# Fetching every token row of an expert block from HBM, one block ahead, in place of picking half of them on chip

## Chip, cores and metric

One core of one Trainium2 chip runs the whole kernel in one launch. The metric is device time in microseconds (us). The kernel before was run three times: 1874.18, 1876.4 and 1895.7 us, median 1876.4 us.

## What is computed

The reference is one layer of a diffusion backbone on 512 latent tokens of width 1024 with 256 context tokens: a mixer (RWKV-7 and HGRN2 heads, output projection, gated residual), then routed and shared SwiGLU experts, another gated residual, and a final RMSNorm. The change lies in the routed experts alone. There, each token goes to 8 of 64 experts, an expert has two 1024x256 matrices (gate, up) and one 256x1024 (down), and the gated results are summed per token:

```python
def _swiglu(x, wg, wu, wd):
    return (jax.nn.silu(x @ wg) * (x @ wu)) @ wd
...
def _moe(h, router_w, router_b, wg, wu, wd, sg, su, sd):
    ...
    _, top_e = lax.top_k(sel, TOP_K)
    gate = jnp.take_along_axis(scores, top_e, axis=1)
    gate = gate / jnp.sum(gate, axis=-1, keepdims=True) * ROUTE_SCALE
    ...
    def step(out, inp):
        tok, gw, e = inp
        y = _swiglu(h[tok], wg[e], wu[e], wd[e]) * gw[:, None].astype(h.dtype)
        return out.at[tok].add(y), None
    routed, _ = lax.scan(step, jnp.zeros_like(h), (tok_buf, gate_buf, blk_e))
    return _swiglu(h, sg, su, sd) + routed
```

Everything is float32; 64 experts of 3 MB each have to be read once.

## The kernel before, in words

The program runs the mixer first (to about 1010 us of the span), then norm, router and shared expert, then the **expert stage**, from about 1095 us to the end.

**Blocks.** Experts are ranked by how many tokens they got; the four experts 0 to 3 of fixed number (NP = 4) come first, since their weights can be loaded before the ranking is known. The work is cut into 46 blocks of at most 128 token rows: a block holds 128 rows of one expert, or 64 rows of each of two, or 96 rows of one and 32 of another. The kinds are interleaved, so three blocks in a row mostly need five experts.

**One block** (the loop over `blocks`, from line 1828):
- `next_list` (`lists`, lines 1621 to 1643) makes the token list of a later block: VectorE (DVE) builds a 0/1 matrix `sel`, four small matmuls and three DVE instructions give the list `lv`, and line 1641 writes it as integers `li` (column 0: rows to read, column 1: rows to add to). There are four `li` buffers, so a new list waits until the scatter that used the list four blocks earlier has landed.
- `front` makes `xT`, the block's token rows transposed and modulated. Most blocks **gather**: GpSimd (POOL) issues an indirect DMA (line 1747) of 128 rows of 4 KB from the DRAM copy `H2_d` into one of two `xg` buffers; TensorE (PE) transposes it with 8 matmuls (line 1753); ScalarE (ACT) writes `xT` (line 1458). The 16 even blocks 12 to 42 (`ONPE`, line 26) instead **pick on chip**: 96 bf16 matmuls (line 1742) multiply `sel` with `h2p`, which holds all 512 rows in three bf16 parts in SBUF.
- `h2_parts` (lines 1725 to 1731) fills `h2p` during blocks 4 to 7 (`HB`): per 128 rows one DMA into an `xg` buffer (`hr`), two ACT copies and two DVE subtractions.
- `ffn_in` (line 1473): 16 to 64 matmuls of 512 columns into `p_gu`. Then `back` for the block before: silu on ACT (1479), product `av` on DVE (1481), transposes on PE (1485), copy on ACT (1487), `ffn_out` (1492) into `p_y`.
- `add_rows`: DVE scales `p_y` into `rows` (1693), POOL issues the indirect **scatter** that adds the 128 rows to `ACC` in DRAM (1694). A scatter waits for the one before it, since both add to the same tensor.

**Weights.** SyncE's queue (SP) carries the loads, three DMAs of 1 MB per expert (line 1378), in the blocks' order. A load is issued only when the second DMA before it has landed (LAG = 2) and when its buffer is free. `wgu` is free after the block's `ffn_in`, `wd` after its `ffn_out`, and those run after the next block's `ffn_in`. Experts 0 to 3 fill the four buffers of pool `wl`; after that line 1717 chooses the pool by a counter:

```python
pl = wl if nload[0] % (NWL + NWR) else wr
nload[0] += 1
```

With NWL, NWR = 4, 1 each load takes the buffer of the expert five loads earlier. A pool hands out its own buffers in turn (`wl` four, `wr` one).

Instruction order on each engine is set by a scheduler from the program's order and its dependences. DVE, POOL, ACT, PE and the SP queue each run their instructions strictly in order.

Of the kernel before, what the change touches and what calls it, by code (L numbers as in the profile page):

```python
# [8 lines left out]
F32 = mybir.dt.float32  # L9
FR = mybir.dt.float32r  # L10
BF = mybir.dt.bfloat16
I32 = mybir.dt.int32
U8 = mybir.dt.uint8
AF = mybir.ActivationFunctionType
OP = mybir.AluOpType
PSUM = bass.MemoryType.PSUM

D = 1024
# [2 lines left out]
NT = SEQ + CTX  # L21
NCH = NT // 64
NCC = CTX // 64
NWL, NWR = 4, 1
LAG = 2
ONPE = range(12, 44, 2)
HB = 4
NP = 4


# [16 lines left out]
def hybrid_layer(ctx, tc, x, c, xctx, c_ctx, w_mod, b_mod, norm1_g, norm2_g, w_in, rw_conv, rw_w0, rw_w2,  # L47
# [3 lines left out]
    nc = tc.nc  # L51
    act, dve, pool, pe = nc.scalar, nc.vector, nc.gpsimd, nc.tensor

    def bc(ap, shape):
        return ap.to_broadcast(shape)
# [17 lines left out]
    def prw(name):  # L73
        turn[0] += 1
        return psb("45"[turn[0] % 2], name)
# [40 lines left out]
    for n in (64, 32):  # L116
        t = const.tile([128, NT // n, n], BF, name=f"rs{n}")
# [100 lines left out]
    sel = const.tile([128, 2], F32)  # L218
# [15 lines left out]
    def dt(name, shape):  # L234
        return dram.tile(list(shape), F32, name=name)
# [13 lines left out]
    H2_d = dt("h2", (NACC, D))  # L249
# [56 lines left out]
    with es:  # L306
        ssx = const.tile([128, 6, 2], F32)
        for t in range(6):
# [6 lines left out]
            for h in range(2):  # L315
                pt = prw("p_xt")
                for q in range(4):
                    kt = h * 4 + q
# [4 lines left out]
        for m in range(4):  # L323
# [3 lines left out]
            for h in range(2):  # L327
                wm = mp.tile([128, 4, 512], F32, name="wm", bufs=4)
                nc.sync.dma_start(wm, dram2(w_mod, m * 512 + h * 512 * 6144, [[6144, 128], [128 * 6144, 4], [1, 512]]))
                for kt in (0, 2, 1, 3):  # L330
                    g = 2 * h + kt // 2
                    pe.matmul(pm[32 * g:32 * g + 32, :], sil[:, 4 * h + kt, :], wm[:, kt, :], start=(kt % 2 == 0),
                              stop=(kt % 2 == 1))
# [887 lines left out]
    def bcast_row(dst, t, off, n):  # L1221
        nc.sync.dma_start(dst, dram2(t, off, [[0, 128], [1, n]]))
# [53 lines left out]
    start = tc.cur_priority  # L1276
# [95 lines left out]
    def load(er, pl):  # L1372

        wgu = pl.tile([128, 2, 2048], F32, name="wgu")
        wd = pl.tile([128, 2048], F32, name="wd")
        for dst, src in ((wgu[:, 0], exp_w_gate), (wgu[:, 1], exp_w_up), (wd, exp_w_down)):
            v = src.rearrange("o e a b -> (o e) (a b)")
            i = nc.sync.dma_start(dst, v[bass.ds(er, 1), :].rearrange("o (p f) -> (o p) f", p=128)).ins

            if len(flight) >= LAG:  # L1380
                tc.add_manual_dep(i, flight[-LAG].name, mybir.DependencyInfo(
                    mybir.DependencyClass.Sync, mybir.DependencyReason.DATA), reason="loads in flight")
            flight.append(i)
        return wgu, wd, i
# [58 lines left out]
    def pst(tag, n, name, w=512):  # L1443
        return psc[0].tile([128, w], F32, name=name, tag=tag, bufs=n)
# [4 lines left out]
    def pss_(tag, name):  # L1449
        psm[tag].append(psm[tag].pop(0))  # L1450
        return psm[tag][-1]

    def modulate(dst, pt, h, eng=act):

        for kt in range(4 * h, 4 * h + 4):
            v = pt[:, (kt - 4 * h) * 128:(kt - 4 * h) * 128 + 128]
            if eng is act:
                act.activation(dst[:, kt, :], v, AF.Identity, scale=s2c[:, kt:kt + 1], bias=sh2c[:, kt:kt + 1])  # L1458
            else:
                dve.tensor_scalar(dst[:, kt, :], v, s2c[:, kt:kt + 1], sh2c[:, kt:kt + 1], op0=OP.mult, op1=OP.add)  # L1460
# [36 lines left out]
    for t in range(4):  # L1497
# [11 lines left out]
        for h in range(2):  # L1509
            pt = pst("pt", 2, "p_h2")  # L1510
# [115 lines left out]
    def lists(parts, kind, rp=RP, rv=RV):  # L1626

        sel = late.tile([128, 4, 128], BF, name="sel", bufs=3)
        pl_ = pss_("li", "p_list")
        p0 = 0  # L1630
        for r, s0, n in parts:
            dve.tensor_tensor(sel[:, :, p0:p0 + n], bc(io[:, None, s0:s0 + n], [128, 4, n]),
                              bc(rp[:, :, r:r + 1], [128, 4, n]), OP.is_equal)
            for t in range(4):
                pe.matmul(pl_[p0:p0 + n, 6 * t:6 * t + 6], sel[:, t, p0:p0 + n], rv[:, t, r], start=True, stop=True)
            p0 += n
        lv = late.tile([128, 8], F32, name="lv", bufs=4)
        dve.tensor_reduce(lv[:, 0:6], pl_[:, 0:24].rearrange("p (t f) -> p f t", t=4), mybir.AxisListType.X, OP.add)
        dve.scalar_tensor_tensor(lv[:, 6:7], lv[:, 2:3], nbp, lv[:, 0:1], op0=OP.mult, op1=OP.add)
        li = late.tile([128, 2], I32, name="li", bufs=4)  # L1640
        dve.scalar_tensor_tensor(li, bc(lv[:, 6:7], [128, 2]), lv[:, 1:2], bpr[:, kind], op0=OP.add, op1=OP.add)  # L1641
        dve.tensor_reduce(lv[:, 7:8], lv[:, 3:6], mybir.AxisListType.X, OP.add)
        return li, lv[:, 7:8], sel


    h64 = lambda a, b: [(a, slice(0, 64)), (b, slice(64, 128))]
# [12 lines left out]
    blocks = [(parts, b, i == 0) for group in order + final for i, (parts, b) in enumerate(group)]  # L1659
    listed = []  # L1660

    def next_list():
        if len(listed) < len(blocks):
            parts, b, _ = blocks[len(listed)]
            s0 = 128 if B2 <= b < BP else 0
            kind = 0 if len(parts) == 1 else 1 if b < BM else 2
            listed.append(lists([(r, s0, s_.stop - s_.start) for r, s_ in parts], kind))
# [33 lines left out]
    wr = fd.enter_context(tc.tile_pool(name="wr", bufs=NWR, side="right", reuse_waits="tile"))  # L1701
    mw = fd.enter_context(tc.tile_pool(name="mw", bufs=2, reuse_waits="tile"))
# [10 lines left out]
    def weights(r):  # L1713

        if r >= 64 - NP:
            return sload[r - 64 + NP][0:2]
        pl = wl if nload[0] % (NWL + NWR) else wr
        nload[0] += 1
        *w, i = load(expert(r), pl)
        last.append(i)  # L1720
        return w

    h2p = mw.tile([128, 3, 4, D], BF, name="h2p", bufs=1)

    def h2_parts(t):

        hr = mw.tile([128, D], F32, name="hr", tag="xg", bufs=2)
        nc.sync.dma_start(hr, H2_d[t * 128:t * 128 + 128, :])
        for i in range(2):
            act.activation(h2p[:, i, t], hr, AF.Copy)  # L1730
            dve.tensor_tensor(hr if i == 0 else h2p[:, 2, t], hr, h2p[:, i, t], OP.subtract)

    def front(tok, sel=None):
        xT = mw.tile([128, 8, 128], F32, name="xT")
        if sel is not None:
            for h in range(2):
                pt = pst("pt", 2, "p_xs")
                for q in range(4):
                    kt = h * 4 + q
                    for i in range(3):  # L1740
                        for t in range(4):
                            pe.matmul(pt[:, q * 128:q * 128 + 128], h2p[:, i, t, kt * 128:kt * 128 + 128], sel[:, t],  # L1742
                                      start=(i == 0 and t == 0), stop=(i == 2 and t == 3))
                modulate(xT, pt, h)
            return xT
        xg = mw.tile([128, D], FR, name="xg", bufs=2)
        pool.indirect_dma_start(out=xg.bitcast(F32), out_offset=None, in_=H2_d,  # L1747
                                in_offset=bass.IndirectOffsetOnAxis(ap=tok, axis=0))
        for h in range(2):
            pt = psc[0].tile([128, 512], FR, name="p_xg", tag="pt", bufs=2)  # L1750
            for q in range(4):
                kt = h * 4 + q
                pe.transpose(pt[:, q * 128:q * 128 + 128], xg[:, kt * 128:kt * 128 + 128], identr)  # L1753
            modulate(xT, pt.bitcast(F32), h)
        return xT
# [69 lines left out]
        nc.sync.dma_start(X_d, xs.rearrange("p i t f -> p (i t f)"))  # L1825

    held = {}
    for i, ((parts, b, first), (li, g, sel)) in enumerate(zip(blocks, listed)):
        if i == 2:
            overflow()  # L1830
        if HB <= i < HB + 4:
            h2_parts(i - HB)
        if i == len(blocks) - 4:
            fr = rows[:, 3]
            bcast_row(fr, final_norm_g, 0, D)
        if first:
            held = {}
        for r, _ in parts:
            if r not in held:
                held[r] = weights(r)  # L1840
        next_list()
        xT = front(li[:, 0:1], sel if i in ONPE else None)
        hv = [(s_, (lambda kt, xT=xT, s_=s_: xT[:, kt, s_]), held[r]) for r, s_ in parts]
        pg = ffn_in(hv, mw)
        if pend:
            back(*pend)
        pend = (pg, hv, g, li[:, 1:2])
# [5 lines left out]
    def extra(i):  # L1853
        er = nc.sync.value_load(xrow[0:1, bass.ds(i, 1)], min_val=0, max_val=63)
        lx = mw.tile([128, 4, 2], F32, name="lx", bufs=1)
        nc.sync.dma_start(lx, X_d[:, bass.ds(i * 8, 8)].rearrange("p (t f) -> p t f", f=2))
        rv = mw.tile([128, 4, 1, 6], BF, name="rv", bufs=1)
        dve.tensor_copy(rv, RV[:, :, 0:1])
        parts3(rv, lx[:, :, 1:2])
        li, g, _ = lists([(0, 0, 128)], 0, lx, rv)  # L1860
        xT, w = front(li[:, 0:1]), load(er, wr)[0:2]
        hv = [(full, lambda kt: xT[:, kt, :], w)]
        back(ffn_in(hv, mw), hv, g, li[:, 1:2])

# [44 lines left out]
```

## Time and profile before

| | |
|---|---|
| profiled execution | 1872.8 us, its span 1871.0 us |
| runs | 1874.18, 1876.4, 1895.7 us |
| PE busy | 1667.0 us (89%), 10155 matmuls |
| DVE, ACT, POOL busy | 751.0, 618.0, 397.2 us |
| granted TensorE clock, mean | 0.896 |
| DMA moved | 401.72 MB, mean 215 GB/s |
| gathers in the expert stage | 30, median 7.7 us to landing |
| scatters | 46, median 11.0 us to landing |

A busy share is a mean over stages with different limits. In the expert stage the slices of the page show which engine is full where; a wait then shows what ended last. Times in the rows count from the span's start.

### The profile page before, as it was taken

Reading aid. Unit: us, or ns where it says so; the run is one execution under the profiler, and the core shown is the slowest. Engines: PE = TensorE matmul, PEld = TensorE weight load, DVE = VectorE, ACT = ScalarE, POOL = GpSimd, SP = SyncE. Lnnn points to the kernel's source line nnn. Section 1 sums busy time; section 2 is a strip of 40 time slices with the busy share of each in tenths; the row PEclk is TensorE's granted clock in tenths of the full one; section 3 lists DMA queues with packets and bytes.
Section 4 is the critical chain, followed back from the end, with each engine's and each line's share of the span. In section 5 each row is a group of like instructions: output and inputs, shape, how many; then the busy total and the mean of one; then the engine's idle time right before and its main releaser. Section 6 shows DMA issues by size and latency. Waiting matters only on the chain. (4 is left out here: it accounts for less than half of the span.)

```text
span 1871.0 us, 26459 instructions
## 1 busy us (share of the span) xinstructions
PE 1667.0 (89%) x10155; PEld 994.6 (53%) x10155; DVE 751.0 (40%) x1722; ACT 618.0 (33%) x1286; POOL 397.2 (21%) x372
## 2 busy tenths in 40 slices
PE   5988989999779999989899997988879999999883
PEld 3756677676567776555445543434334544454431
DVE  3665595755847335433344633311112121212113
ACT  5464435426224435342132423321112222222121
POOL 2234222313313124232123011210111111111111
PEclk9976899989867997868799998998889999999997
DMA  7323445546456435453443688799997899999995
GB/s 267 92 59 100 136 136 156 166 112 171 131 152 186 147 119 172 145 171 118 131 146 119 252 302 272 248 322 334 343 302 252 300 339 343 339 328 333 341 340 169
DMA packets 200256, 401.72 MB, mean 215 GB/s; under 512 B 41804, under 2 KB 132009, under 8 KB 175168
## 3 DMA queue, kind: packets, MB, share of 16 engines
q1 hardware_dynamic: 188768, 360.05, 55.9%
q0 software_dynamic: 11360, 39.96, 9.6%
q8 instruction: 81, 1.33, 0.3%
q14 instruction: 47, 0.39, 0.1%
HBM read 323.66 MB, written 73.15 MB: 212 GB/s over the span
## 5 line engine op out<-in xcount | busy, mean ns | idle before, releaser
L1473 PE MATMUL p_gu<-wgu,xT 128*32 128x512 f32 (+2 forms) x1424 | 353.7, 621 | 16.6 <-DMA wgu<-in_exp_w_up_dram 15.9
L1473 PEld LDWEIGHTS p_gu<-wgu,xT 128*32 128x32 f32 (+2 forms) x1424 | 125.9, 143 | 202.4 <-issue 178.9
L1492 PE MATMUL p_y<-wd,at 128*32 128x512 f32 (+2 forms) x744 | 198.0, 621 | 4.8 <-ACT at L1487 3.6
L369 PE MATMUL p_proj<-hTh,w_hi 128*128 128x512 f32 (+1 forms) x456 | 183.3, 402 | 6.0 <-ACT w_hi L296 3.1
L370 PE MATMUL p_proj<-hTh,w_lo 128*128 128x512 f32 (+1 forms) x456 | 177.3, 390 | 3.6 <-DVE w_lo L298 3.6
L371 PE MATMUL p_proj<-hTl,w_hi 128*128 128x512 f32 (+1 forms) x456 | 177.2, 390 | 2.9 <-POOL hTl L351 2.2
L1641 DVE SCALAR_TENSOR_TENSOR li<-lv,bpr 128x2 int32<-128x2 f32 x46 | 10.1, 219 | 411.3 <-DMA acc<-rows,li 299.8
L1694 POOL DMA_INDIRECT acc<-rows,li x46 | 74.3, 1615 | 371.1 <-DVE rows L1693 336.8
L1479 ACT ACTIVATE sl<-p_gu 128x256 f32<-128x256 f32 x50 | 19.1, 383 | 330.5 <-PE p_gu L1473 329.0
L1492 PEld LDWEIGHTS p_y<-wd,at 128*32 128x32 f32 (+2 forms) x744 | 66.3, 147 | 102.1 <-issue 89.2
L1458 ACT ACTIVATE xT<-p_xg,sh2c,s2c 128x128 f32<-128x128 f32 x240 | 89.6, 460 | 91.0 <-PE p_xg L1753 90.8
L369 PEld LDWEIGHTS p_proj<-hTh,w_hi 128*128 128x128 f32 x456 | 94.9, 208 | 28.5 <-issue 6.6
L1693 DVE SCALAR_TENSOR_TENSOR rows<-p_y,lv,g2r 128x512 f32<-128x512 f32 x92 | 67.2, 745 | 100.4 <-PE p_y L1492 100.4
L371 PEld LDWEIGHTS p_proj<-hTl,w_hi 128*128 128x128 f32 x456 | 94.6, 208 | 22.1 <-issue 5.4
L370 PEld LDWEIGHTS p_proj<-hTh,w_lo 128*128 128x128 f32 x456 | 94.7, 208 | 19.5 <-issue 4.9
L1747 POOL DMA_INDIRECT xg<-h,li x30 | 31.0, 1034 | 344.5 <-issue 108.1
L1742 PE MATMUL p_xs<-sel,h2p 128*128 128x128 bf16 x1536 | 92.9, 219 | 0.0
L1742 PEld LDWEIGHTS <-h2p 128*128 128x128 bf16 x1536 | 87.3, 98 | 9.0 <-issue 8.6
L687 PE MATMUL p_sc<-AR,BK 64*128 64x128 f32 (+1 forms) x384 | 64.2, 334 | 20.9 <-DVE SC L689 10.1
L1458 ACT ACTIVATE xT<-p_xs,sh2c,s2c 128x128 f32<-128x128 f32 x128 | 48.1, 457 | 89.9 <-PE p_xs L1742 89.9
L687 PEld LDWEIGHTS p_sc<-AR,BK 64*128 64x128 f32 x384 | 49.8, 221 | 42.4 <-DVE SC L689 14.0
L298 DVE TENSOR_TENSOR w_lo<-w_raw,w_hi 128x1024 fp32r<-128x1024 f32 x35 | 46.3, 1323 | 42.4 <-ACT w_hi L296 42.4
(520 smaller groups left out, 2695.7 us busy)
## 6 DMA issues: line engine op xcount, KB each, us to landing
wgu<-in_exp_w_gate_dram SPq DMA_DIRECT2D x64, 1024.0 KB, 7.5
wgu<-in_exp_w_up_dram SPq DMA_DIRECT2D x64, 1024.0 KB, 7.5
wd<-in_exp_w_down_dram SPq DMA_DIRECT2D x64, 1024.0 KB, 6.4
w_raw<-in_w_in_dram SPq DMA_DIRECT2D x35, 512.0 KB, 4.1
wm<-in_w_mod_dram SPq DMA_DIRECT2D x32, 512.0 KB, 4.0
pkt<-pk SPq DMA_DIRECT2D x24, 576.0 KB, 4.2
wm<-in_w_mod_dram SPq DMA_DIRECT2D x8, 1024.0 KB, 5.2
pk<-SC SPq DMA_DIRECT2D x32, 256.0 KB, 3.1
```

Source lines behind the costliest of these rows:

```text
L298: dve.tensor_tensor(wl, w, wh.bitcast(F32), OP.subtract)
L369: pe.matmul(o[k], wh[:, kt, :], hTh[:, kt, s], start=(kt == 0), stop=False)
L370: pe.matmul(o[k], wl[:, kt, :], hTh[:, kt, s], start=False, stop=False)
L371: pe.matmul(o[k], wh[:, kt, :], hTl[:, kt, s], start=False, stop=(kt == 7))
L687: pe.matmul(p3[:, i], bk[r, n + i, :], ar[r, n + i, 0:w], start=True, stop=True)
L1458: act.activation(dst[:, kt, :], v, AF.Identity, scale=s2c[:, kt:kt + 1], bias=sh2c[:, kt:kt + 1])
L1473: pe.matmul(pg[r], lhs(kt)[:, o:o + r.stop - r.start], w[0][:, :, kt * 256:kt * 256 + 256], start=(kt == 0), stop=(kt == 7))
L1492: pe.matmul(py[n][r], at[:, t * 128 + r.start:t * 128 + r.stop], w[1][:, t * 1024 + n * 512:t * 1024 + n * 512 + 512], start=(t == 0), sto ...
L1693: dve.scalar_tensor_tensor(yo[:, cs_], py[n], g, g2r[:, cs_], op0=OP.mult, op1=OP.mult)
L1694: pool.indirect_dma_start(out=ACC if two else ACC[0:NACC], in_=yo, in_offset=None, compute_op=OP.add, out_offset=bass.IndirectOffsetOnAxis ...
L1742: pe.matmul(pt[:, q * 128:q * 128 + 128], h2p[:, i, t, kt * 128:kt * 128 + 128], sel[:, t], start=(i == 0 and t == 0), stop=(i == 2 and t ...
L1747: pool.indirect_dma_start(out=xg.bitcast(F32), out_offset=None, in_=H2_d, in_offset=bass.IndirectOffsetOnAxis(ap=tok, axis=0))
```

## The change

The on-chip picking goes: `ONPE`, `HB`, `h2p`, `h2_parts` and the branch of `front` with the 96 matmuls. All 46 blocks gather. The gather moves out of `front` into `fetch`, and the loop calls it for block i+1 before it calls `front` for block i. The space of `h2p` (24 KB per partition) becomes a second buffer of pool `wr` (NWR = 2); the counter of line 1717 then runs modulo 6. `xg` keeps two buffers, `li` four.

```diff
-NWL, NWR = 4, 1
+NWL, NWR = 4, 2
 LAG = 2
-ONPE = range(12, 44, 2)
-HB = 4
 NP = 4
...
-        return li, lv[:, 7:8], sel
+        return li, lv[:, 7:8]
...
-    h2p = mw.tile([128, 3, 4, D], BF, name="h2p", bufs=1)
-
-    def h2_parts(t):
-
-        hr = mw.tile([128, D], F32, name="hr", tag="xg", bufs=2)
-        nc.sync.dma_start(hr, H2_d[t * 128:t * 128 + 128, :])
-        for i in range(2):
-            act.activation(h2p[:, i, t], hr, AF.Copy)
-            dve.tensor_tensor(hr if i == 0 else h2p[:, 2, t], hr, h2p[:, i, t], OP.subtract)
-
-    def front(tok, sel=None):
-        xT = mw.tile([128, 8, 128], F32, name="xT")
-        if sel is not None:
-            for h in range(2):
-                pt = pst("pt", 2, "p_xs")
-                for q in range(4):
-                    kt = h * 4 + q
-                    for i in range(3):
-                        for t in range(4):
-                            pe.matmul(pt[:, q * 128:q * 128 + 128], h2p[:, i, t, kt * 128:kt * 128 + 128], sel[:, t],
-                                      start=(i == 0 and t == 0), stop=(i == 2 and t == 3))
-                modulate(xT, pt, h)
-            return xT
+    def fetch(tok):
+
         xg = mw.tile([128, D], FR, name="xg", bufs=2)
         pool.indirect_dma_start(out=xg.bitcast(F32), out_offset=None, in_=H2_d,
                                 in_offset=bass.IndirectOffsetOnAxis(ap=tok, axis=0))
+        return xg
+
+    def front(xg):
+        xT = mw.tile([128, 8, 128], F32, name="xT")
         for h in range(2):
...
+    fetched = [fetch(listed[0][0][:, 0:1])]
-    for i, ((parts, b, first), (li, g, sel)) in enumerate(zip(blocks, listed)):
+    for i, ((parts, b, first), (li, g)) in enumerate(zip(blocks, listed)):
...
-        if HB <= i < HB + 4:
-            h2_parts(i - HB)
...
+        if i + 1 < len(blocks):
+            fetched.append(fetch(listed[i + 1][0][:, 0:1]))
         next_list()
-        xT = front(li[:, 0:1], sel if i in ONPE else None)
+        xT = front(fetched[i])
```

Two places show what the scheduler makes of it. On POOL, in the middle of the expert stage (`xg` is a gather, `acc` a scatter), the kernel before has:

```order
L1694 DMA acc<-rows,li 1280x1024 x2
L1747 DMA xg<-h_219,li 128x1024
L1694 DMA acc<-rows,li 640x1024 x2
L1747 DMA xg<-h_219,li 128x1024
L1694 DMA acc<-rows,li 1280x1024
```

and the changed one:

```order
L1724 DMA xg<-h_219,li 128x1024
L1692 DMA acc<-rows,li 640x1024
L1724 DMA xg<-h_219,li 128x1024
L1692 DMA acc<-rows,li 1280x1024
L1724 DMA xg<-h_219,li 128x1024
```

Where two scatters followed each other, a gather now stands between any two. In the stretch of the kernel before in which every block gathers, the same alternation stands already.

On DVE, near block 12 (`li` is a written list, `av` the product that PE waits for, `rows` the scaled output of an earlier block), the kernel before has:

```order
L1641 SCALAR_TENSOR_TENSOR li<-lv,bpr 128x2
L1693 SCALAR_TENSOR_TENSOR rows<-p_y_9266,lv,g2r 128x512
L1638 TENSOR_REDUCE lv<-p_bank 128x6
L1639 SCALAR_TENSOR_TENSOR lv<-lv,nbp 128x1
L1642 TENSOR_REDUCE lv<-lv 128x1
L1641 SCALAR_TENSOR_TENSOR li<-lv,bpr 128x2
L1481 TENSOR_TENSOR av<-sl,p_gu 128x128x2
```

and the changed one:

```order
L1639 SCALAR_TENSOR_TENSOR li<-lv,bpr 128x2
L1691 SCALAR_TENSOR_TENSOR rows<-p_y_9126,lv,g2r 128x512
L1691 SCALAR_TENSOR_TENSOR rows<-p_y_9127,lv,g2r 128x512
L1630 TENSOR_TENSOR sel<-io,RP 128x4x64
L1636 TENSOR_REDUCE lv<-p_bank 128x6
L1630 TENSOR_TENSOR sel<-io,RP 128x4x64
L1637 SCALAR_TENSOR_TENSOR lv<-lv,nbp 128x1
L1640 TENSOR_REDUCE lv<-lv 128x1
L1639 SCALAR_TENSOR_TENSOR li<-lv,bpr 128x2
L1479 TENSOR_TENSOR av<-sl,p_gu 128x128x2
```

In both, two lists stand between one `av` and the next, so here an `av` waits behind two scatters.

## Rows read from the trace of the kernel before

**Rows 1.** The page: span, and the span in 40 slices (46.8 us each).

```profile
span 1871.0 us, 26459 instructions
PE   5988989999779999989899997988879999999883
...
DMA  7323445546456435453443688799997899999995
GB/s 267 92 59 100 136 136 156 166 112 171 131 152 186 147 119 172 145 171 118 131 146 119 252 302 272 248 322 334 343 302 252 300 339 343 339 328 333 341 340 169
```

**Rows 2.** Stretches of the expert stage: us, engines' busy us (instructions), clock, DMA share, GB/s.

```profile
1100.00:1250.00 150.00, 128.74 (x524) 59.30 (x523) 43.75 (x121) 45.00 (x110) 24.51 (x18) 0.93 0.85 285
1250.00:1350.00 100.00, 82.49 (x629) 40.36 (x630) 16.75 (x45) 21.05 (x57) 11.26 (x8) 0.88 0.98 337
1350.00:1500.00 150.00, 137.62 (x934) 65.90 (x936) 27.60 (x73) 30.00 (x84) 18.75 (x13) 0.95 0.87 289
1500.00:1800.00 300.00, 282.91 (x2086) 137.63 (x2084) 60.77 (x162) 72.19 (x197) 40.56 (x29) 0.97 0.98 338
```

**Rows 3.** The same view for tile p_xs alone: PE busy, ACT busy.

```profile
1250.00:1350.00 100.00, 17.78 (x288) 9.01 (x24) 0.88 0.98 337
1350.00:1500.00 150.00, 23.09 (x384) 12.01 (x32) 0.95 0.87 289
1500.00:1800.00 300.00, 52.07 (x864) 27.04 (x72) 0.97 0.98 338
```

**Rows 4.** SP queue's waits, 1260 to 1480, then 1480 to 1810: us, times, longest.

```profile
SPq L1378 <- PE p_bank L1635: 19.5, 3, 11.5
SPq L1378 <- PE p_gu L1473: 9.2, 3, 8.9
...
SPq L1378 <- DMA wd<-in_exp_w_down_dram: 100.0, 30, 6.2
SPq L1378 <- PE p_y L1492: 0.8, 2, 0.6
```

**Rows 5.** PE's waits, 1260 to 1480, then 1480 to 1836.

```profile
PE p_bank L1485 <- DVE av L1481: 25.2, 5, 8.4
...
PE p_gu L1473 <- DMA wgu<-in_exp_w_up_dram: 15.9, 6, 5.7
```

**Rows 6.** The page's DMA queues: packets, MB, share of 16 engines' span.

```profile
q1 hardware_dynamic: 188768, 360.05, 55.9%
q0 software_dynamic: 11360, 39.96, 9.6%
```

**Rows 7.** Timelines of ACT, DVE, POOL in blocks 2 to 4: start, us, engine.

```profile
1127.37 1.06 ACT L1730 ACTIVATE h2p<-hr 128x1024 bf16<-128x1024 f32 x1 [7.71 <-DMA hr<-h]
...
1180.51 0.22 DVE L1641 SCALAR_TENSOR_TENSOR li<-lv,bpr 128x2 int32<-128x2 f32 x1 [6.90 <-DMA acc<-rows,li]
...
1186.58 1.58 POOL L1694 DMA_INDIRECT acc<-rows,li  x1 [0.30 <-issue]
```

**Rows 8.** Timelines of DVE and POOL where every block gathers.

```profile
1209.87 0.22 DVE L1641 SCALAR_TENSOR_TENSOR li<-lv,bpr 128x2 int32<-128x2 f32 x1 [12.36 <-DMA acc<-rows,li]
1225.22 0.22 DVE L1641 SCALAR_TENSOR_TENSOR li<-lv,bpr 128x2 int32<-128x2 f32 x1 [12.44 <-issue]
...
1210.83 0.98 POOL L1747 DMA_INDIRECT xg<-h,li  x1 [12.29 <-PE p_y L1492]
1212.11 1.58 POOL L1694 DMA_INDIRECT acc<-rows,li  x1 [0.30 <-DVE rows L1693]
1257.52 1.75 POOL L1694 DMA_INDIRECT acc<-rows,li  x1 [14.09 <-DVE rows L1693]
...
1836.18 1.55 POOL L1694 DMA_INDIRECT acc<-rows,li  x1 [9.91 <-DVE rows L1693]
```

**Rows 9.** PE's timeline: transposes of one gathered block; and PE's waits for gathers.

```profile
1102.85 1.21 PE L1753 MATMUL p_xg<-identr,xg 128*128 128x128 f32 x8
...
PE p_xg L1753 <- DMA xg<-h,li: 20.8, 9, 4.8
```

More of the change, by code (lines that the diff above doesn't have):

```diff
@@ L1859, in extra @@
         parts3(rv, lx[:, :, 1:2])
-        li, g, _ = lists([(0, 0, 128)], 0, lx, rv)
-        xT, w = front(li[:, 0:1]), load(er, wr)[0:2]
+        li, g = lists([(0, 0, 128)], 0, lx, rv)
+        xT, w = front(fetch(li[:, 0:1])), load(er, wr)[0:2]
         hv = [(full, lambda kt: xT[:, kt, :], w)]
```

## The prediction

> **What bounds the kernel now.** First the page's slices: until about 1030 us the DMA engines are mostly half idle or more; from about 1075 us (slice 23, counted from 0) to the last slice they stand at 7 to 9 tenths, and PE is at 7 to 9 as well [rows 1]. The change touches only that part, so I read it by stretches [rows 2]. From 1250 to 1350 and from 1500 to 1800 the DMA share is 0.98 at 337 and 338 GB/s: full. From 1100 to 1250 it is 0.85 and from 1350 to 1500 it is 0.87, so 22.5 and 19.5 us of DMA time stand idle there. Then who waits for whom. From 1480 on the load queue waits 100.0 us for one kind of earlier DMA alone and hardly at all for PE, and PE waits 15.9 us for weights [rows 4, 5]: there the loads set the pace. From 1260 to 1480 the queue does wait for PE, 28.7 us in 6 waits, 4.8 us each [rows 4]: a buffer is not free, because PE itself stood 25.2 us for `av` [rows 5].
>
> Why does `av` come late? DVE takes its work in order, and the new list `li` stands ahead of `av` and `rows`. At 1209.87 a list is written, after 12.36 us of waiting for a scatter; `rows` follow; the next scatter starts at 1212.11, 2.24 us after the list; the next list can be written at 1225.22 [rows 8]. So scatter, list, rows, scatter is a ring of 15.35 us a block. From the tenth scatter, at 1257.52, to the 45th, at 1836.18, 35 blocks take 578.7 us, 16.5 each [rows 8]. The ring is a little under that pace, the loads are at it, and PE has some slack: three limits lie close together, and this is what makes a small change uncertain.
>
> **The change, part by part.** The sum is made against the profiled execution, 1872.8 us (1871.0 of span and 1.8 around it); it stands 3.6 us under the median of the runs, 1876.4, and 1.4 under the lowest. I don't correct for that.
>
> *Sixteen gathers more.* 16 blocks pick on chip now: 288, 384 and 864 picking matmuls in the three stretches [rows 3], at 96 a block, are 3, 4 and 9 blocks. Each becomes a gather of 128 rows of 4 KB, 0.524 MB. Twelve of them fall where the DMA is full. The lower price of one is its bytes at the rate of a full stretch: 0.524 MB / 338 GB/s = 1.55 us. The upper comes from the queues: the software queue, which carries gathers and scatters, took 9.6% of 16 engines' span for 39.96 MB, 179.6 us or 4.5 us a MB, where the load queue took 2.9 [rows 6]; so 2.36 us for 0.524 MB. Scatters, which also read what they add to, are in that mean and may carry most of the excess, so I take the middle, 1.95 us, and 12 x 1.95 = **+23.4 us** (18.6 to 28.3). The four in the slack stretch need 7.8 us and are hidden by its 19.5 us of idle DMA; without that cover they too would cost.
>
> The Trainium skill (DMA: Bandwidth & Descriptors, "Anatomy of one DMA — SWDGE (gpsimd) path") has another price for a DMA issued by GpSimd: about 2.0 us that don't load the engines, plus bytes over 436 GB/s. By it the twelve would cost 14.4 us instead of 23.4 (an estimate from that page). The trace speaks against it: no full stretch moves more than 338 GB/s [rows 2].
>
> *The picking itself.* PE loses 92.9 us of matmuls [rows 3] and gains 16 x 1.21 = 19.4 us of transposes [rows 9], so 73.5 us less. I take **0** on the end for it: twelve of the sixteen lie under full DMA, which covers PE. The ACT writes of `xT` stay, from another tile.
>
> *Four loads of `hr` and the making of `h2p`.* This is in the first slack stretch, which blocks pass one behind the other. ACT stood 7.71 us for the first of these loads [rows 7], with a silu and the writes of `xT` queued behind. DVE's subtractions stand between list and scatter: 1180.51 to 1186.58 is 6.07 us [rows 7], against 2.24 later [rows 8], and two blocks show this, 3.8 us each. At most 7.7 + 7.6 = 15.3 us, if nothing else is late then; the next late thing is the scatter in the ring, which stays. I take half, **-7.7 us** (-15.3 to 0). It counts at the end, since idle DMA there means that later loads move up by as much. The 2.1 MB of `hr` lie in idle DMA time and give nothing.
>
> *The gather a block ahead.* **0.** On POOL gather and scatter alternate exactly as they already do where every block gathers, and a gather still follows the list which waits for a scatter: 1210.83 after 1209.87 [rows 8]. The program order moves; the wait does not. PE's waits for gathers (20.8 us in the whole stage [rows 9]) stay.
>
> *Idle DMA from 1350 to 1500.* After the four gathers 11.7 us are left. PE's stops for `av` come from two lists ahead of one `av`; the order of the change still has such places, but not the same ones. I take half, **-5.9 us** (-11.7 to 0).
>
> *The buffer.* The counter now runs modulo 6, but it sends five of six loads to the four buffers of `wl`, and one in six to the two of `wr`. Numbering from 0 the 60 loads that the counter sees: load 5 takes the buffer of load 1, four earlier; load 6 takes a free one; loads 7 to 10 again the one five earlier; load 11 that of load 7, four earlier. So nothing is prefetched deeper (the load with the spare buffer stands in the queue behind the late one), and ten loads, 5, 11, ... 59, wait for one expert more than now. The trace has no such load. Its price is 0 where the loads are at the DMA's pace anyway, and at most a whole wait of a load for PE, 4.8 us [rows 4]. By the times of the loads the first falls where the DMA is idle anyway (0), four between 1260 and 1480: half a wait, 2.4 each; five later, where the costliest such wait is 0.4 us (0.8 in 2 [rows 4]). 9.6 + 2.0 = **+11.6 us** (0 to 9 x 4.8 = 43.2).
>
> Sum: 23.4 - 7.7 - 5.9 + 11.6 = +21.4, so 1872.8 + 21.4 = **1894 us**, 0.9% above the median.
>
> **Rivals.**
> - *The gathers are hidden.* If the share of 0.98 still has room (packets of two queues filling each other's gaps), the twelve cost nothing, and the slack is won: -7.7 - 11.7, 1853 us. For it: PE is 94% busy from 1500 to 1800 [rows 2], so PE may be as much of a bound. Against: PE waited for weights there, not they for PE.
> - *Fetching ahead works.* If gathers are early enough, PE's 20.8 us of waits for them go [rows 9], and the sum is +0.6: 1873 us. Against it stands the order on POOL. The Trainium skill (the same page, "Rules for kernel authors") advises it: issue the DMA early, wait late, so that the fixed cost overlaps. By that rule this rival would hold.
> - *PE was the bound.* Then its 73.5 us go: 1799 us. The full DMA share speaks against it; so many bytes more in so much less time are hard to see.
> - *Scatters slow down behind gathers.* The ring takes over once a scatter needs more than 578.7 / 35 - 2.24 = 14.3 us from issue to the next list; now that is up to 13.1 with a gather ahead of it [rows 8]. At 15.3, 35 x 1.0 = 35 us more, less the 7.7: 1900 us.
> - *The buffers decide.* If each of nine late loads holds the queue a whole wait, the buffer term is 43.2: 23.4 - 7.7 - 5.9 + 43.2 = +53, **1926 us**, slower than now by 2.6%. It decides from about 3.6 us a load. For it: in three blocks five experts are needed and two blocks' weights are held at once, so four buffers leave no room ahead. Against: from 1480 on the queue hardly waits for PE.
>
> **How the numbers follow.** Chances: my forecast 0.50, its own range 1875 to 1912; gathers hidden 0.17; fetching ahead 0.07; PE the bound 0.03; scatters 0.10; buffers 0.13. The predicted time is the forecast's, 1894. The range takes in the ends of the unknown prices, and leaves out PE the bound, the outer half of the hidden case and most of the buffers' case: 1860 to 1922, about 0.2 outside. Two per cent, about what a measurement of this kernel can tell from no change, is 37.5 us: faster means under 1839, slower over 1914. Faster: PE the bound and a tail of the hidden case, 0.05. Slower: the buffers' case and the upper tails of the forecast and of the scatters, 0.17. Within: 0.78.
>
> **What would show it.** Gathers: the DMA share at 0.97 or more from 1250 to 1800 without the dip of 1350 to 1500, and PE's wait for weights well above 15.9 us. Early part: no ACT wait of 7 us near 1127, and the tenth scatter some 8 us before 1257.5. Buffers: the load queue's waits for PE longer than now, at every sixth expert. Fetching ahead: PE's waits for gathers near 20 us mean that it did nothing. The scatters: more than 14.3 us between a scatter and the next list. I am wrong if the DMA share falls below 0.95 in the later part: then a ring or the buffers set the pace, not the bytes.

## The result: slower by 3%, and outside the range

The changed kernel takes **1935.6 us** (median of 4 runs, 1929.0 to 1954.2) against 1879.1 for the kernel before (1874.2 to 1895.7): a ratio of **1.030 [1.020, 1.040]**. I had said 1894, in a range of 1860 to 1922, and gave a loss of over 2% a chance of 0.17. The profiled execution of the change took 1933.4 us. Some runs of a kernel come out over 1.5% longer than its fastest one; ratios, and the medians of the experiments, leave them out.

The page of the changed kernel, the lines that answer to [rows 1]; a slice is now 48.3 us:

```profile
span 1931.6 us, 23649 instructions
...
PE   5998899999699999898999989687698677876583
...
DMA  7314445544564453534434887999979979889955
GB/s 258 98 51 126 142 131 165 165 135 127 140 197 145 131 186 116 181 116 153 141 127 180 313 288 223 329 350 334 306 257 346 337 284 329 277 274 320 316 187 164
```

Its stretches, with the columns of [rows 2]:

```profile
1100.00:1250.00 150.00, 125.95 (x538) 56.77 (x536) 37.85 (x121) 38.78 (x107) 25.42 (x19) 0.93 0.87 282
1250.00:1350.00 100.00, 75.93 (x382) 27.48 (x382) 16.63 (x43) 19.30 (x55) 13.44 (x10) 0.85 0.95 339
1350.00:1500.00 150.00, 118.14 (x568) 46.28 (x568) 27.64 (x78) 29.58 (x83) 24.15 (x19) 0.92 0.90 306
1500.00:1800.00 300.00, 216.62 (x1040) 83.34 (x1040) 49.50 (x134) 57.09 (x159) 41.44 (x32) 0.85 0.90 304
```

The late part, full before (0.98, 338 GB/s), is at 0.90 and 304 GB/s, and PE is busy 217 us of 300 there instead of 283. So neither the bytes nor PE's work set the pace: both wait. What for, PE's waits and then SyncE's queue's say (us, times, longest; PE over 1045 to 1930, the queue from 1480 to 1870):

```profile
PE p_xg L1734 <- DMA xg<-h,li: 107.0, 17, 13.7
PE p_bank L1483 <- DVE av L1479: 58.9, 14, 7.2
...
PE p_gu L1471 <- DMA wgu<-in_exp_w_up_dram: 2.5, 2, 1.9
```

```profile
SPq L1376 <- PE p_bank L1633: 24.5, 4, 11.6
SPq L1376 <- PE p_y L1490: 22.7, 4, 12.1
SPq L1376 <- PE p_gu L1471: 10.9, 3, 7.0
```

PE's waits for gathered rows were 20.8 us [rows 9] and are 107.0; those for `av` went from 25.2 [rows 5] to 58.9; those for weights from 15.9 [rows 5] to 2.5. The order has turned round: the loads now wait for PE, where from 1480 on they had hardly done so [rows 4].

Where in time it was lost: the tenth scatter starts at 1238.34, 19.2 us earlier than before [rows 8], the 45th at 1896.40, 60.2 later. The 35 blocks between them take 658.1 us instead of 578.7, 18.8 each instead of 16.5. These two scatters in POOL's timeline:

```profile
1238.34 1.57 POOL L1692 DMA_INDIRECT acc<-rows,li  x1 [1.96 <-DVE rows L1691]
...
1896.40 1.55 POOL L1692 DMA_INDIRECT acc<-rows,li  x1 [9.91 <-DVE rows L1691]
```

One turn of it, in the timelines of DVE, POOL and PE of the changed kernel (start, us; in brackets the idle time ahead and what ended it):

```profile
1358.31 0.22 DVE L1639 SCALAR_TENSOR_TENSOR li<-lv,bpr 128x2 int32<-128x2 f32 x1 [5.29 <-DMA acc<-rows,li]
1358.45 0.74 DVE L1691 SCALAR_TENSOR_TENSOR rows<-p_y,lv,g2r 128x512 f32<-128x512 f32 x1
...
1373.64 0.22 DVE L1639 SCALAR_TENSOR_TENSOR li<-lv,bpr 128x2 int32<-128x2 f32 x1 [13.49 <-DMA acc<-rows,li]
1373.78 0.59 DVE L1479 TENSOR_TENSOR av<-sl,p_gu 128x256 f32<-128x256 f32 x1
...
1348.45 1.77 POOL L1692 DMA_INDIRECT acc<-rows,li  x1 [13.89 <-DVE rows L1691]
1359.27 1.11 POOL L1724 DMA_INDIRECT xg<-h,li  x1 [9.05 <-issue]
1360.69 1.58 POOL L1692 DMA_INDIRECT acc<-rows,li  x1 [0.30 <-issue]
...
1384.04 1.64 POOL L1692 DMA_INDIRECT acc<-rows,li  x1 [8.45 <-DVE rows L1691]
...
1368.66 1.26 PE L1734 MATMUL p_xg<-identr,xg 128*128 128x128 f32 x8 [7.63 <-DMA xg<-h,li]
1374.42 0.69 PE L1483 MATMUL p_bank<-ident,av 128*128 128x128 f32 x2 [4.50 <-DVE av L1479]
```

The scatter issued at 1348.45 has to land before the list can be written, 9.9 us later (`li` has four buffers, and the scatter still reads the oldest). Only then does the gather go out, at 1359.27, and PE gets its rows at 1368.66 after 7.63 us of standing. The next scatter, at 1360.69, holds the next list until 1373.64; `av` is behind that list on DVE, and PE stands 4.50 us for it. PE's `p_y` comes after both, then `rows`, then the scatter at 1384.04. From 1348.45 to 1384.04 two blocks took 35.6 us.

**Theory A**, the list ring: scatter, list, gather, PE, rows, scatter, now with the gather's landing and PE in it for every block. Before, the sixteen picked blocks opened it: their rows came out of `sel`, which needs no scatter, and the page of the kernel before shows no idle time at all ahead of its picking matmuls:

```profile
L1742 PE MATMUL p_xs<-sel,h2p 128*128 128x128 bf16 x1536 | 92.9, 219 | 0.0
```

**Rivals:** B, the weight buffers (the late loads of the prediction). C, the sixteen gathers' bytes and their queue.

A fourth reading is the clock: PE's mean granted clock from 1500 to 1800, as a share of full speed, is 0.97 before and 0.85 after. The first experiment bears on it.

### The profile page after: what moved, and what is told of

It reads as the page before. It is cut to its first block, busy times and chain, and to the rows that moved or that the text cites. A ratio compares the mean times of both kernels' runs of the same rounds, so it can differ in the third digit from the quotient of the medians.

```text
span 1931.6 us, 23649 instructions
## 1 busy us (share of the span) xinstructions
PE 1620.8 (84%) x8747; PEld 924.9 (48%) x8747; DVE 740.8 (38%) x1714; ACT 607.7 (31%) x1278; POOL 412.7 (21%) x388
## 5 line engine op out<-in xcount | busy, mean ns | idle before, releaser
L1471 PE MATMUL p_gu<-wgu,xT 128*32 128x512 f32 (+2 forms) x1424 | 359.7, 612 | 2.7 <-DMA wgu<-in_exp_w_up_dram 2.5
L1490 PE MATMUL p_y<-wd,at 128*32 128x512 f32 (+2 forms) x744 | 218.9, 653 | 12.6 <-ACT at L1485 11.6
L1456 ACT ACTIVATE xT<-p_xg,sh2c,s2c 128x128 f32<-128x128 f32 x368 | 138.2, 465 | 155.1 <-PE p_xg L1734 154.9
L1477 ACT ACTIVATE sl<-p_gu 128x256 f32<-128x256 f32 x50 | 19.2, 384 | 452.8 <-PE p_gu L1471 451.3
L1724 POOL DMA_INDIRECT xg<-h,li x46 | 46.1, 1003 | 509.4 <-issue 305.4
L1734 PE MATMUL p_xg<-identr,xg 128*128 128x128 f32 x368 | 50.7, 276 | 107.0 <-DMA xg<-h,li 107.0
L1734 PEld LDWEIGHTS p_xg<-identr,xg 128*128 128x128 f32 x368 | 40.0, 151 | 125.0 <-DMA xg<-h,li 75.4
L1483 PE MATMUL p_bank<-ident,av 128*128 128x128 f32 x92 | 23.6, 332 | 60.8 <-DVE av L1479 58.9
L1479 DVE TENSOR_TENSOR av<-sl,p_gu 128x256 f32<-128x256 f32 x50 | 30.1, 601 | 105.4 <-ACT sl L1477 105.4
```

The source lines that it names most:

```text
L1471: pe.matmul(pg[r], lhs(kt)[:, o:o + r.stop - r.start], w[0][:, :, kt * 256:kt * 256 + 256], start=(kt == 0), stop=(kt == 7))
L1479: dve.tensor_tensor(av.rearrange("s t p -> s p t"), sl.rearrange("s (p t) -> s p t", t=2), pg[:, 256:512].rearrange("s (p t) -> s p t", t= ...
L1490: pe.matmul(py[n][r], at[:, t * 128 + r.start:t * 128 + r.stop], w[1][:, t * 1024 + n * 512:t * 1024 + n * 512 + 512], start=(t == 0), sto ...
```

## Experiments

Each was timed against the kernel before in the same session, where that one's median lay between 1870 and 1881 us. The ratio to it stands with its 95% interval; it need not be the quotient of two medians.

### Eight lists instead of four

```
-        lv = late.tile([128, 8], F32, name="lv", bufs=4)
+        lv = late.tile([128, 8], F32, name="lv", bufs=8)
...
-        li = late.tile([128, 2], I32, name="li", bufs=4)
+        li = late.tile([128, 2], I32, name="li", bufs=8)
```

> The changed kernel with eight buffers instead of four for the list tiles li and lv; nothing else. Theory A (list ring: a list is written only when the scatter of the list four blocks earlier has landed, the gather follows the list, PE follows the gather): the lists run ahead, PE's 107 us of waits for gathered rows fall below 40 and the time falls from 1936 to 1875-1915. Theory B (weight buffers: every sixth load waits for an expert one too near): no change, 1928-1944. Theory C (the sixteen gathers' bytes): no change either.

1868.7 us, 0.9946 [0.9902, 0.9989] of the kernel before: the whole loss is gone with 40 bytes a partition per extra list. The stretches, and PE's waits:

```profile
1350.00:1500.00 150.00, 132.77 (x622) 52.27 (x622) 29.32 (x79) 33.46 (x94) 24.49 (x19) 0.90 0.98 332
1500.00:1800.00 300.00, 235.19 (x1181) 89.41 (x1180) 54.05 (x142) 62.77 (x176) 47.11 (x35) 0.91 0.97 338
```

```profile
PE p_xg L1734 <- DMA xg<-h,li: 84.2, 14, 11.1
PE p_gu L1471 <- DMA wgu<-in_exp_w_up_dram: 18.2, 8, 4.9
PE p_bank L1483 <- DVE av L1479: 15.6, 14, 1.2
```

The time fell as A had it, to a little under its 1875; the wait didn't: 84.2 us where I expected under 40. The DMA is full from 1350 to 1800 (0.98, 0.97), so PE has to stand somewhere, and standing for rows need cost nothing then. The size of a wait is no measure of its price. The clock of the late stretch is 0.91, still under the 0.97 of the kernel before, and nothing is lost: a clock under 0.97 does not by itself cost the 3%. What did vanish is the list's own wait. The rows below give the waits in DVE's queue ahead of the list's line from 1260 to 1870 (ns, least/median/most), in the changed kernel and then with eight lists:

```profile
L1639 DVEq EVENT_SEMAPHORE  x32: 49/9884/13545, 1261.5 to 1853.8; - x32
```

```profile
L1639 DVEq EVENT_SEMAPHORE  x31: 21/21/21, 1282.2 to 1786.1; - x31
```

### Five lists

`bufs=4` of `li` becomes 5; `lv` stays.

> The changed kernel with five li buffers instead of four. Theory A (list ring): the list waits for the scatter five blocks earlier, one block more of slack (about 17 us against a scatter's landing of 9 to 15), so most of what eight buffers gave comes with the fifth: 1870-1900. If it is eight lists' order of instructions and not the wait that helped (rival), 1915-1940.

1867.5 us, 0.997 [0.992, 1.002], just under A's 1870. One block of slack is enough: DVE's waits for the list from 1260 to 1870 are 21 us in 7, where the change has 293 in 30. The scheduler's order moves with the buffers, mainly where PE's transposes of gathered rows stand, and five lists have another order than eight (17 places on PE), so it is not one particular order that helps. But both also differ from the change's order (18 and 17 places), and no run holds the order fixed while it adds a buffer: what part the order has in the gain is not shown.

### Loads dealt to the weight buffers six by six

```
-        pl = wl if nload[0] % (NWL + NWR) else wr
+        pl = wl if nload[0] % (NWL + NWR) >= NWR else wr
```

> The changed kernel with its loads dealt to the buffers in rows of six (two in the pool of two, four in the pool of four), so that every load reuses the buffer of the load six earlier instead of now four, now twelve. Theory A (list ring): no change beyond 10 us, 1926-1946, since the loads already run ahead of PE. Theory B (weight buffers): SyncE's waits for PE after 1480 us, 58 us now, fall below 15 and the time by 15 to 45 us, to 1890-1920. Theory C (bytes): no change.

1931.0 us, 1.031 [1.022, 1.040], the same as the change. B is out as the cause of the loss.

### The bytes without the wait

In the kernel before, ahead of the picking in `front`:

```
         if sel is not None:
+            xg = mw.tile([128, D], FR, name="xg", bufs=2)
+            pool.indirect_dma_start(out=xg.bitcast(F32), out_offset=None, in_=H2_d,
+                                    in_offset=bass.IndirectOffsetOnAxis(ap=tok, axis=0))
```

> The kernel before, picking its sixteen blocks on chip as it does, with a gather of the same rows added in each of these blocks into a buffer that nothing reads: the bytes and POOL's work of the change without PE waiting for them. Theory A (list ring): the bytes cost at most the 23 us of the prediction, 1880-1902. Theory C (the sixteen gathers' bytes and their queue): at least 40 us, 1919-1940.

1882.5 us, 2 over the kernel before and inside A's 1880 to 1902. This rests on two runs, 1881.9 and 1883.1, and has no interval; the two left out took 1914.2 and 1919.1 (all four have a median of 1898.6). C's 1919 to 1940 is not met by either measure, so C falls. PE waits for the loads here, as the prediction had thought of the change:

```profile
PE p_gu L1473 <- DMA wgu<-in_exp_w_up_dram: 33.1, 8, 8.2
PE p_bank L1485 <- DVE av L1481: 28.8, 5, 8.4
PE p_xg L1756 <- DMA xg<-h,li: 18.0, 6, 7.1
```

### The switch alone

`ONPE = range(12, 44, 2)` of the kernel before becomes `ONPE = ()`.

> The kernel before with the list of on-chip blocks emptied: all 45 blocks gather, still in their own turn, with five weight buffers and the twelve loads and conversions of h2p left in. Theory A (list ring): this alone carries the loss, 1920-1955, with PE's waits for gathered rows at 80 us or more. Theory B (the sixth buffer's order): only the bytes are left, 1890-1905. Theory C (bytes): 1920-1945 too, but with PE's waits for weights up instead of its waits for rows.

1947.8 us (1944.5 to 1963.8), 1.041 [1.031, 1.051], inside A's range. It has the bytes, lists, buffers and loads of the experiment above; the one difference in kind is that PE picks nothing and waits for the sixteen gathers. That makes **65 us** between the medians (57 with every run counted, the figure in an expectation below), and the runs of the two don't overlap, whichever are counted. The change, without `hr` loads, with the fetch ahead and the sixth buffer, stands 0.011 below it, give or take 0.014: not told apart.

### The same two with eight lists

Both kernels with `bufs=8` for `li` and `lv`.

> The kernel before with its sixteen picks, a gather that nothing reads added in each, and eight li and lv buffers: the gathers' bytes alone with the lists free. Against the kernel before with eight lists (0.9917 of the kernel before) the bytes cost what the prediction said, 15 to 28 us: 1875-1890. If the loss of the added gathers with four lists was partly their scatters' and lists' (rival), under 10 us: 1858-1870.

> The kernel before with all 45 blocks gathered in their own turn, h2p's loads left in, and eight li and lv buffers: what the emptied list of on-chip blocks costs when the lists run free. Theory A: the 57 us that PE's wait for these gathers cost with four lists shrink below 15 us against the same bytes with picks, 1875-1900. If the wait for a gather costs as such and not through the list (rival), 1905-1945.

With the added gathers 1873.7 us, 0.998 [0.995, 1.002]; with the switch 1864.3 us, 0.993 [0.988, 0.998]. The 65 us between them are gone (now -9): waiting for a gather doesn't cost as such, it costs through the list. The first fell just under its range of 1875 to 1890, and the second 11 us under 1875. This is the table on which that rests, medians in us:

| | 16 gathers beside the picks | 16 gathers in place of the picks |
|---|---|---|
| four lists | 1882.5 | 1947.8 |
| eight lists | 1873.7 | 1864.3 |

### Gather late, or DVE held up?

The list has two columns, the gather's and the scatter's indices. Here the gather's get a tile of their own (`fetch` reads `gi`), `lv` has eight buffers, and `li` still waits:

```
-        lv = late.tile([128, 8], F32, name="lv", bufs=4)
+        lv = late.tile([128, 8], F32, name="lv", bufs=8)
...
+        gi = late.tile([128, 1], I32, name="gi", bufs=8)
+        dve.scalar_tensor_tensor(gi, lv[:, 6:7], lv[:, 1:2], bpr[:, kind, 0:1], op0=OP.add, op1=OP.add)
         li = late.tile([128, 2], I32, name="li", bufs=4)
```

> The changed kernel with the gather's indices in a tile of their own (gi, eight buffers, one small DVE operation more for each block), written ahead of li; li keeps its four buffers and still waits for the scatter four blocks earlier. Theory A1 (what is late is the gather, for want of its list): the time comes back as with eight lists, 1865-1895. Theory A2 (what is late is everything behind li on DVE, av and rows above all): the time stays, 1915-1945, with PE's waits for av at 40 us or more.

1879.6 us, 1.007 [1.002, 1.012], inside A1's range. The late gather (A1) carries most: 0.023 (give or take 0.011) of the 0.036 between the change and eight lists, with what the order of PE and ACT adds. The rest, 0.012, goes with `li` still holding up DVE, and with the added operation; this run doesn't part these two. PE's and ACT's order is that of eight lists, so their order doesn't explain this rest. DVE's waits from 1260 to 1870 show that the list stood as long as ever, and PE's that it mattered little:

```profile
DVE li L1641 <- DMA acc<-rows,li: 263.0, 31, 11.8
```

```profile
PE p_xg L1736 <- DMA xg<-h,gi: 78.5, 14, 10.3
PE p_bank L1483 <- DVE av L1479: 31.7, 13, 5.5
```

### Does the kernel before have the ring?

The same `bufs=8` in the kernel before.

> The kernel before with eight buffers instead of four for li and lv; it still picks sixteen blocks on chip. If the picks already broke the list ring there (theory A as it stands), little is left to gain: the DMA idles 7% of 1260-1870 us before, so at most some 20 us, 1860-1882. If the ring cost the kernel before as much as the changed one (rival), 1815-1850.

1859.6 us, 0.992 [0.987, 0.997], at the lower edge of what I expected. The kernel before loses about 0.8% to it (0.3 to 1.3), though its lists waited for scatters just as long. DVE's waits there, from 1260 to 1870:

```profile
DVE li L1641 <- DMA acc<-rows,li: 240.7, 24, 14.0
DVE li L1641 <- issue: 86.0, 9, 12.1
```

That is 327 us in 33 blocks; in the changed kernel it is 293 in 30 (86.2 for scatters, 206.9 under "issue", which is time that the profile puts down to nothing). With eight lists neither kernel has either kind any more. The wait had been there all along. The picks kept it from PE.

### Fetching ahead, and the buffers, once the lists are free

Eight lists and the gather in its own block again (`xT = front(fetch(li[:, 0:1]))`, no `fetched`); then that with the loads six by six; then that with `NWR = 1`, five buffers and the counter as it was.

> The changed kernel with eight li and lv buffers, and with each gather written in its own block again, not a block ahead. If fetching ahead was worth nothing (as the prediction had it), 1862-1880, as with eight lists alone. If the gather a block ahead is what lets the lists' slack be used (rival), 1890-1930 with PE's waits for rows above 110 us.

> The changed kernel with eight li and lv buffers, gathers in their own block, and loads dealt to the six weight buffers in proper rotation (every load reuses the buffer of the load six earlier). If the DMA engines are the limit once the lists run free (theory A), the buffers' order is worth under 8 us: 1852-1872. If the buffers' order was hidden under the ring and is now the next wait (theory B), 1835-1852.

> The changed kernel with eight li and lv buffers, gathers in their own block, and five weight buffers instead of six (the space left empty). Theory A with the DMA as the limit: the sixth buffer is worth little, 1855-1878. If the sixth buffer is what pays now (rival), 1880-1900, with SyncE's waits for PE above 60 us.

In its own block: 1862.2 us, 0.996 [0.991, 1.000], against 0.995 with the fetch a block ahead; on PE, DVE, ACT and POOL the two have the same instructions in the same order, so the move is nothing at all, and their 6 us of medians are what runs differ by. Six buffers in rotation: 1854.0 us, 0.984 [0.975, 0.994]. Five buffers: **1845.1 us, 0.984 [0.975, 0.994]**, under its own range of 1855 to 1878. So a sixth buffer in rotation shows no gain over five. But the change's own way of dealing, five loads to one pool and one to the other, stands 0.011, give or take 0.011, above both (0.996): once the lists are free it may cost about 1%. SyncE's waits for PE from 1045 to 1870 speak for that in part: 44 us with it, 5 with six in rotation, 27 with five. The even dealings had three and four runs, so this stays open. The kernel with five, without picks and `hr`, is ahead of both the kernel before and the change. Its stretches:

```profile
1100.00:1250.00 150.00, 138.01 (x643) 60.34 (x645) 42.53 (x132) 43.44 (x121) 28.99 (x23) 0.97 0.96 327
1250.00:1350.00 100.00, 76.23 (x356) 28.11 (x357) 16.59 (x43) 19.30 (x55) 13.39 (x10) 0.86 0.97 348
1350.00:1500.00 150.00, 131.08 (x668) 51.29 (x665) 31.12 (x85) 35.21 (x99) 26.95 (x20) 0.93 0.99 341
1500.00:1800.00 300.00, 238.78 (x1147) 90.74 (x1146) 52.44 (x137) 61.31 (x172) 44.05 (x33) 0.90 0.95 328
```

Here the DMA is at 0.95 or more from 1100 to 1800. It had four runs, so by the interval it is 0.6 to 2.5% faster than the kernel before, and it isn't told apart from eight lists in the kernel before (0.992).

## Why the prediction was wrong, step by step

- **The step that failed: "The program order moves; the wait does not. PE's waits for gathers (20.8 us in the whole stage [rows 9]) stay."**, with the **0** for the picking beside it. The list's wait did stay; PE's waits for gathers did not, they rose to 107.0 us. I took 20.8 us over although sixteen blocks were about to join it, and I priced the picks by PE's work alone (73.5 us under full DMA). Their worth was that every second block got its rows without a list. Replacing them cost 65 us with four lists and nothing with eight.
- **"The ring is a little under that pace."** The 15.35 us were read where scatter, list, rows and scatter follow closely. In the changed kernel the gather's landing and PE stand between list and rows: 18.8 a block. The rival with the scatters had the ring take over, and I gave it 0.10, but with another cause (scatters slower behind gathers). From 1260 to 1800 a scatter took 11.0 us from issue to landing in the median before, and 10.9 in the change; it is not slower.
- **Gathers' bytes, +23.4 (18.6 to 28.3).** With eight lists, 0.998 against 0.992: 12 us, give or take 11; with four, 2 by two runs. Direction right, rather too large. Why is not shown: with the added gathers and eight lists the stretches at 0.96 and 0.97 moved 326 to 338 GB/s, no more than the 337 and 338 that I took for full.
- **`hr` and `h2p`, -7.7 (-15.3 to 0).** From first to tenth scatter the stage took 140.7 us before (1116.86 to 1257.52) and 127.2 after (1111.18 to 1238.34): -13.5, near its far end. The kernel of 0.984 with five buffers differs from the switch with eight lists (0.993) only by these: -17 us, give or take 20.
- **The gather a block ahead, 0.** Right, and shown with eight lists; with four it was not run alone. In the change the gather went out right after its list (1359.27 after 1358.31), and the list waited for a scatter: what is written a block earlier was not issued earlier. The Trainium skill (DMA: Bandwidth & Descriptors, "Rules for kernel authors") advises to issue a DMA early and wait for it late; in no pair of runs here does writing it ahead alone give an earlier issue, so none shows what that would give.
- **Idle DMA, -5.9 (-11.7 to 0).** From 1350 to 1500 the share rose from 0.87 to 0.90, 4.5 us, while the full stretch after it lost 24 (0.98 to 0.90 of 300).
- **The buffer, +11.6 (0 to 43.2).** With four lists 0 (1.030 and 1.031). SyncE's waits for PE from 1480 on (58 us of the rows above) looked like it, but with eight lists, dealt as in the change, 2 us of them are left. With eight lists the term is open: 21 us, give or take 20, between the change's dealing and either even one. The rival whose time was nearest (1926) had the wrong cause for the loss and came near by luck.
- **"I am wrong if the DMA share falls below 0.95 in the later part: then a ring or the buffers set the pace, not the bytes."** It fell to 0.90, and it was a ring.
- **Two slips that move nothing.** In the last slice the DMA stands at 5 tenths and PE at 3, not at 7 to 9; and the buffers' case decides from 3.5 us a load, not 3.6: (1914 - 1872.8 - 9.8) / 9, with 9.8 for the other three terms.

## To carry to other kernels

Ask of every piece of work that a change removes what it does not wait for: work that needs no transfer lets an engine run on while a chain of small waits turns, and that chain is not seen as long as it does. A wait of 327 us on an engine that is no bottleneck is a warning when the change makes more readers follow it. Where a tile of a few bytes is released by a transfer that lands 10 us later, count its buffers in blocks of slack, and give it one more before anything is reordered.

## What was not expected of the hardware

A gather took longer to land where the time was shorter. POOL's issues from 1260 to 1800, median us from issue to landing, for the changed kernel and then with eight lists:

```profile
acc<-rows,li POOLq DMA_INDIRECT x30, 10.9
xg<-h,li POOLq DMA_INDIRECT x29, 7.0
```

```profile
acc<-rows,li POOLq DMA_INDIRECT x32, 10.8
xg<-h,li POOLq DMA_INDIRECT x31, 12.4
```

12.4 us instead of 7.0, while scatters are the same in both. The share alone doesn't make it (0.97 here, 0.91 there, but 7.5 us at 0.95 in the kernel before). With eight lists every gather of that time goes out about 2 us behind a scatter (POOL's timeline, with eight lists, below); in the changed kernel none of the 29 does, and in the turn shown above it went ahead of one. The same holds in the kernel before: with four lists none of its 17 gathers starts within 3 us after a scatter and they land in 7.5 us, with eight all 17 do and land in 12.1, at shares of 0.95 and 0.96. So the place behind a scatter goes with the longer landing in every kernel that was profiled; that it is the cause was not tried apart from the lists.

```profile
1534.21 1.86 POOL L1692 DMA_INDIRECT acc<-rows,li  x1 [23.86 <-DVE lv L1636]
1536.37 0.98 POOL L1724 DMA_INDIRECT xg<-h,li  x1 [0.30 <-issue]
```

And a full share has no one rate: with the indices split, the stretch from 1250 to 1350 moved 365 GB/s, where the full stretches before moved 337 and 338 [rows 2]:

```profile
1250.00:1350.00 100.00, 70.96 (x338) 27.40 (x332) 16.65 (x47) 17.55 (x50) 13.66 (x10) 0.84 1.00 365
```
